# A down-projection with seven of 22 row-block pairs in Strassen's seven-product scheme, and the first norm's scale and shift during the up-projection

## The chip, the cores and the metric

One core of one Trainium2 chip runs one hybrid decoder layer for 256 tokens of 2048 channels. The metric is the time of one execution in microseconds (us) on the device. TensorE is written PE, VectorE DVE, ScalarE ACT, GpSimd POOL; SP issues most transfers.

## The reference, cut to what matters

The part of the layer that the change touches is its second half:

```python
x = layer_norm(DN_ALPHA * x + mix, ln1_g[l], ln1_b[l])
x = layer_norm(DN_ALPHA * x + conv_ffn(x, w_up[l], conv_w[l], conv_b[l], w_down[l]), ln2_g[l], ln2_b[l])
...
def layer_norm(x, g, b):
    ...
    y = (xf - mu) * lax.rsqrt(var + LN_EPS) * g + b

def conv_ffn(x, w_up, conv_w, conv_b, w_down):
    h = x @ w_up
    ...                      # acc: causal depthwise convolution of width 3 on h
    a, b = jnp.split(acc, 2, axis=-1)
    return (jax.nn.silu(a) * b) @ w_down
```

The tokens are 2 halves of 128. w_up is 2048 x 11264, w_down 5632 x 2048, all in float32.

## The kernel before, in words

Every product is made of three matmuls on parts with fewer mantissa bits: a number is split into hi and lo (`split`: ACT writes hi by a copy, DVE writes lo = value - hi), and the product is x_hi w_hi + x_hi w_lo + x_lo w_hi. Weights come from HBM in transfers of 1 MB on SP's queue into `raw` (2 buffers). `pieces` yields them in halves of 1024 columns per partition: ACT writes `whi` (line L70), DVE `wlo` (L74), 4 buffers each, and PE multiplies. The order of PE's instructions is the order of the code. Those of ACT, DVE, POOL and SP are put in order by a scheduler when the program is built, with a priority for what stands under `hp()`; at run time each engine takes its instructions strictly in that order. In the stretch around the first norm the order of ACT and DVE is the written one.

The stages at the end of the program:

- First norm and its turn (about 843 to 860 us): `ln1_turn` transposes 512 columns of the normalised x1 on PE, applies scale and shift along the partitions, and writes hi (ACT) and lo (DVE, `ln1_low`) into x1T, the operand of the up-projection. PE meanwhile does the first block of the up-projection in halves, and has to have the lo of (token half 1, part c) before it can do the matmuls of part c.
- Up-projection (to about 1340 us): 22 values of j, two products of 256 columns each (`feat_major`), then the convolution (`cv`), silu, and the split of the result into `aT`.
- Down-projection (1340 to 1580 us): four blocks of 512 columns (`tok_major`). In each, 44 row blocks of 128 are taken two to a piece; each row block takes 2 token halves x 3 matmuls of 512 columns. In the last block the last 12 row blocks are first done for token half 0, and then for token half 1 in two steps of 256 columns (`ENDS`), so that the second norm of half 0 lies beside the matmuls of half 1.
- x1 in its row form needs the first norm's scale and shift too, since it is added in the second norm. At the start of the down-projection two transfers of 1 MB on POOL's queue bring them to all partitions (`gb1`), and 8 multiplications and 8 additions of 128 x 512 on DVE apply them. Two more transfers of 1 MB bring those of the second norm (`g2`).
- `gb1` and `g2` lie in the memory of x1T (tiles x1T1 and x1T0), which is free when the last matmul of the up-projection is done.

## Time and profile before

| | |
|---|---|
| median of 3 runs | 1592.53 us (1592.27 to 1593.0) |
| the profiled execution's own time | 1593.32 us |
| its span in the trace | 1591.2 us |
| PE busy | 1576.0 us, 99% of the span |
| DVE busy | 1006.1 us, 63% |
| ACT busy | 835.9 us, 53% |
| read from HBM | 301.71 MB, 191 GB/s over the span |

The span is what the hardware profiler recorded from the first instruction to the last; the execution's own time is 2.1 us longer. Busy shares are of the span. An instruction's duration on PE and DVE overlaps that of the next a little, so the cost of one in a chain is the distance between two starts.

### The profile page before, as it was taken

The page shows a single profiled execution, that of the slowest core. Times are in us where ns is not written, and L with a number is a line of the kernel's source. Part 1 is how long each engine was busy: PE and PEld are TensorE (multiplying, and loading weights), DVE is VectorE, ACT ScalarE, POOL GpSimd, SP SyncE. Part 2 cuts the span into 40 slices and gives each one's busy share as a digit, 9 for nine tenths or more (in the row PEclk, how much of TensorE's full clock was granted, in tenths as well). Part 3 has the DMA queues.
Part 4 walks back from the last instruction along what each step waited for, and adds up shares of the span by engine and source line. Part 5 has one row for each costly group of instructions (what it writes and reads, how often), then busy time and mean ns, then how long its engine had stood idle before and what let it go on. Part 6 is the DMA issues. An engine that isn't in the chain of part 4 may idle for free.

```text
span 1591.2 us, 20296 instructions
## 1 busy us (share of the span) xinstructions
PE 1576.0 (99%) x8129; PEld 1343.7 (84%) x8129; DVE 1006.1 (63%) x1214; ACT 835.9 (53%) x986; POOL 30.2 (2%) x100
## 2 busy tenths in 40 slices
PE   9999999999999999999999999999999999999997
PEld 7888888888888888888889888888888888888886
DVE  5776547765448766447566666667666766654455
ACT  5555448546458555444447555555555555434332
POOL 1200000000000000000000000000000000000001
PEclk9999999999999999999999999999999999999999
...
GB/s 249 233 185 198 186 187 170 199 184 160 187 186 182 189 181 170 200 185 185 238 212 126 193 194 191 195 188 186 185 186 192 193 193 273 207 193 201 187 188 129
DMA packets 215645, 305.10 MB, mean 192 GB/s; under 512 B 5116, under 2 KB 133684, under 8 KB 215040
## 3 DMA queue, kind: packets, MB, share of 16 engines
...
HBM read 301.71 MB, written 2.10 MB: 191 GB/s over the span
## 4 chain that ended last, share of the span: by engine, by line
PE 97%; DMA 1%; DVE 1%; ACT 0%; SPq 0%; issue 0%
PE mm L108 30%; PE mm L150 17%; PE mm L151 16%; PE mm L149 16%; PE mm L111 15%; PE ax L554 1%; DMA raw<-in_w_out_dram 1%; PE mm L132 1%; DMA y<-in_w_in_dram 1%; DVE x L67 0%; PE mm L134 0%; PE ax L736 0%; PE ax L516 0%; DVE klo L74 0%; PE ax L425 0%; PE ax L672 0%
## 5 line engine op out<-in xcount | busy, mean ns | idle before, releaser
L74 DVE TENSOR_TENSOR wlo<-raw,whi 128x1024 fp32r<-128x1024 f32 x538 | 653.9, 1221 | 512.5 <-ACT whi L70 511.6
L70 ACT ACTIVATE whi<-raw 128x1024 fp32r<-128x1024 f32 x538 | 564.9, 1056 | 649.3 <-PE mm L151 264.3
L108 PE MATMUL mm<-x1T,whi 128*128 128x512 f32 x1376 | 432.2, 395 | 0.0
L111 PEld LDWEIGHTS mm<-x1T,wlo 128*128 128x128 f32 x1376 | 258.5, 188 | 61.1
L111 PE MATMUL mm<-x1T,wlo 128*128 128x256 f32 x1376 | 270.3, 278 | 0.0
L149 PE MATMUL mm<-whi,X 128*128 128x512 f32 x608 | 237.9, 391 | 0.0
L151 PE MATMUL mm<-whi,X 128*128 128x512 f32 x608 | 236.6, 389 | 0.0
L150 PE MATMUL mm<-wlo,X 128*128 128x512 f32 x608 | 236.6, 389 | 0.0
L108 PEld LDWEIGHTS mm<-x1T,whi 128*128 128x128 f32 x1376 | 209.4, 189 | 0.0
L108 PE MATMUL mm<-X,whi 128*128 128x512 f32 x640 | 201.9, 397 | 1.3 <-DVE X L74 1.3
L111 PEld LDWEIGHTS mm<-X,wlo 128*128 128x128 f32 x640 | 120.2, 188 | 28.4
L149 PE MATMUL mm<-whi,aT 128*128 128x512 f32 (+1 forms) x352 | 135.2, 384 | 0.0
L150 PE MATMUL mm<-wlo,aT 128*128 128x512 f32 (+1 forms) x352 | 135.2, 384 | 0.0
L151 PE MATMUL mm<-whi,aT 128*128 128x512 f32 (+1 forms) x352 | 135.2, 384 | 0.0
L151 PEld LDWEIGHTS mm<-whi,X 128*128 128x128 f32 x608 | 114.1, 188 | 23.9
L150 PEld LDWEIGHTS mm<-wlo,X 128*128 128x128 f32 x608 | 114.2, 188 | 23.1
L149 PEld LDWEIGHTS mm<-whi,X 128*128 128x128 f32 x608 | 114.2, 188 | 23.1
L111 PE MATMUL mm<-X,wlo 128*128 128x256 f32 x640 | 125.9, 278 | 0.0
L108 PEld LDWEIGHTS mm<-X,whi 128*128 128x128 f32 x640 | 97.8, 189 | 2.0 <-DVE X L74 1.7
L149 PEld LDWEIGHTS mm<-whi,aT 128*128 128x128 f32 x352 | 66.1, 188 | 13.2
L151 PEld LDWEIGHTS mm<-whi,aT 128*128 128x128 f32 x352 | 66.1, 188 | 13.2
L150 PEld LDWEIGHTS mm<-wlo,aT 128*128 128x128 f32 x352 | 66.1, 188 | 12.9
...
## 6 DMA issues: line engine op xcount, KB each, us to landing
raw<-in_w_in_dram SPq DMA_DIRECT2D x100, 1024.0 KB, 5.0
raw<-in_w_up_dram SPq DMA_DIRECT2D x88, 1024.0 KB, 5.1
raw<-in_w_down_dram SPq DMA_DIRECT2D x44, 1024.0 KB, 5.1
raw<-in_w_out_dram SPq DMA_DIRECT2D x16, 1024.0 KB, 5.1
raw<-in_w_pool_proj_dram SPq DMA_DIRECT2D x8, 1024.0 KB, 5.1
raw<-in_w_sg_proj_dram SPq DMA_DIRECT2D x8, 1024.0 KB, 5.1
raw<-in_w_hg_proj_dram SPq DMA_DIRECT2D x8, 1024.0 KB, 5.0
y<-in_w_in_dram SPq DMA_DIRECT2D x3, 1024.0 KB, 13.0
```

The source lines that it names most:

```text
L70: nc.scalar.activation(out=o, in_=a, func=f, **kw)
L74: low.tensor_tensor(out=lo, in0=src, in1=hi.bitcast(F32), op=ALU.subtract)
L108: nc.tensor.matmul(ps[:, c, :], lhsT=hi[:, k, c * P:(c + 1) * P], rhs=xT(kt)[:, 0:512], start=kt == 0, stop=False)
L111: nc.tensor.matmul(ps[:, c, 0:256], lhsT=lo[:, k, c * P:(c + 1) * P], rhs=xT(kt)[:, 0:256], start=False, stop=kt == kt_n - 1)
L132: nc.tensor.matmul(pv[:, :, ts], lhsT=hi[:, k, cs], rhs=xv[:, :, ts], start=kt == 0, stop=False)
L149: nc.tensor.matmul(o[:, w], lhsT=xT(kt)[:, xs], rhs=hi[:, k, w], start=kt == first, stop=False)
L150: nc.tensor.matmul(o[:, w], lhsT=xT(kt)[:, xs], rhs=lo[:, k, w], start=False, stop=False)
L151: nc.tensor.matmul(o[:, w], lhsT=xT(kt)[:, xl], rhs=hi[:, k, w], start=False, stop=kt == kt_n - 1)
L554: nc.tensor.matmul(tp[:, hc], lhsT=ke[:, hc], rhs=qe[:, hc], start=True, stop=True)
```

## The change: what it does

The down-projection is done in two quads of 1024 columns. Two row blocks of weights (k = 0, 1) by two halves of columns (h = 0, 1) are a pair: a 2 x 2 block matrix, multiplied by the 2 x 2 block matrix of activations (2 token halves by 2 row blocks). A plain pair takes 8 block products of 3 matmuls, 24 in all. The 7 pairs in `FAST` take 7 products, 21 matmuls, in each quad, with sums of activations (`mix_tokens`, made once, in the first quad) and sums of weights (`tt`, in each quad). Three of the seven products and one more are gathered in accumulators of their own (`e`) and added to x1 by `drain`; the rest go straight into the accumulators of the result (`c`), which `settle` adds to x1. `ORDER0` and `ORDER1` say in which order PE takes the pairs. The first quad has all 22 pairs; the second has 16 by this scheme and the last 12 row blocks as before, with the same ending by `ENDS`. A pair's weights are 1 MB; a third place for them, `wide[:, 1]`, and the place of the weights' sums, `wide[:, 0]`, lie in x1T1. The activations' sums lie in x1T0 for four pairs and in a new pool for three, so `g2` can be loaded into x1T0 only when PE is done with the fourth fast pair (pair 6) in the second quad.

The scale and shift of x1 are now written in the up-projection, for j = 4 to 11, in 8 slices of 256 columns with two transfers of 128 KB on POOL's queue and four DVE operations each, in one buffer `gb`.

```diff
+TAIL = 16
+FAST = (0, 2, 4, 6, 8, 10, 12)
+ORDER0 = (1, 3, 0, 5, 7, 2, 9, 11, 4, 13, 14, 6, 15, 16, 8, 17, 18, 10, 19, 12, 20, 21)
+ORDER1 = (1, 0, 3, 2, 5, 4, 7, 6, 9, 8, 11, 10, 13, 12, 14, 15)
...
+    def ln1_affine(i):
+        cs = slice(256 * i, 256 * (i + 1))
+        gb = pas.tile([P, 2, 256], F32, name="gb", bufs=1)
+        nc.gpsimd.dma_start(out=gb[:, 0, :], in_=ln1_g[0, cs].partition_broadcast(P))
+        nc.gpsimd.dma_start(out=gb[:, 1, :], in_=ln1_b[0, cs].partition_broadcast(P))
+        for t in range(NT):
+            mul(x1[:, t, cs], x1[:, t, cs], gb[:, 0, :])
+            add(x1[:, t, cs], x1[:, t, cs], gb[:, 1, :])
...
     for j in range(KF // 2):
+        if 4 <= j < 12:
+            ln1_affine(j - 4)
...
-    g2 = ff.tile([P, 2, D], F32, name="x1T0")
-    gb1 = ff.tile([P, 2, D], F32, name="x1T1")
-    nc.gpsimd.dma_start(out=gb1[:, 0, :], in_=ln1_g[0].partition_broadcast(P))
-    nc.gpsimd.dma_start(out=gb1[:, 1, :], in_=ln1_b[0].partition_broadcast(P))
-    for c in range(4):
-        cs = slice(512 * c, 512 * (c + 1))
-        for t in range(NT):
-            mul(x1[:, t, cs], x1[:, t, cs], gb1[:, 0, cs])
-            add(x1[:, t, cs], x1[:, t, cs], gb1[:, 1, cs])
...
-    for j in range(3):
-        cs = slice(512 * j, 512 * (j + 1))
-        ps = tok_major(wdown, 512 * j, aT, KF)
...
+    def mix_tokens(p):
+        with hp():
...
+            add(work[:, 0:512].rearrange("p (j c) -> p j c", j=2), av[:, :, 0:S], av[:, :, S:2 * S])
+            sub(sm[:, 1, :], full[:, 0, 0, :], full[:, 0, 1, :])
+            sub(sm[:, 0, :], full[:, 1, 1, :], full[:, 0, 1, :])
+            add(sm[:, 2, :], full[:, 0, 0, :], sm[:, 0, :])
+            sub(sm[:, 3, :], full[:, 1, 0, :], sm[:, 2, :])
+            to = S_of(p)
+            split(to[:, 0], to[:, 1], sm)
...
+    def quarters(p, cb):
...
+            if i % 3 == 2:
+                raw = wide[:, 1].rearrange("p (k h) c -> p k (h c)", k=2)
+            else:
+                raw = wst.tile([P, 2, 1024], F32, name="raw", bufs=RAW_BUFS)
+            nc.sync.dma_start(out=raw, in_=wdv[:, 2 * p:2 * p + 2, cb:cb + 1024])
...
+    def plain_pair(p, cb, c):
+        q = quarters(p, cb)
+        for j in range(2):
+            w2, w1 = both(q[:, 2 * j:2 * j + 2, :])
+            for i in range(NT):
+                x = act_of(p, j, i)
+                c[i, 2].go(x, w2)
+                c[i, 1].go(x, w1)
+
+    def fast_pair(p, cb, c, e):
...
+        b11, b22 = both(q[:, 1:3, :])
+        with hp():
+            tt = wide[:, 0]
+            add(tt[:, 0:2, :], q[:, 1:3, :], q[:, 0:1, :].broadcast_to([P, 2, 512]))
+            add(tt[:, 2, :], tt[:, 0, :], q[:, 2, :])
+            add(tt[:, 3, :], tt[:, 2, :], q[:, 3, :])
+        e[1].go(act_of(p, 0, 0), b11)
+        c[0, 2].go(s4, b22)
+        b21, = both(q[:, 3:4, :], 1)
+        c[0, 1].go(act_of(p, 1, 0), b21)
+        t1, t3 = both(tt[:, 0:2, :])
+        e[5].go(s5, t1)
+        e[7].go(s7, t3)
+        t2, t4 = both(tt[:, 2:4, :])
+        e[6].go(s6, t2)
+        c[1, 1].go(act_of(p, 1, 1), t4)
...
+    def settle(cb, t, n, ps):
+        with hp():
+            v = at(cb, t, n)
+            add(v, v, ps)
+            nc.vector.bn_stats(out=st2[:, t, cb // 512 + 2 - n, :], in_=v)
...
+            if p in FAST:
+                fast_pair(p, cb, c, e)
+                todo -= 1
+                if not quad and todo:
+                    mix_tokens(FAST[NF - todo])
+                if not todo:
+                    drain(cb, e)
+            else:
+                plain_pair(p, cb, c)
+        if not quad:
+            for t in range(NT):
+                for n in (2, 1):
+                    settle(cb, t, n, c[t, n].ap)
+    g2 = ff.tile([P, 2, D], F32, name="x1T0")
```

Where the scheduler put the instructions is seen in the built programs. Names carry buffer numbers; line numbers differ between the two programs (lo was L74 and is L78, subtraction L58 and L62, addition L61 and L65, multiplication L64 and L68).

**The first norm's turn, on DVE.** Before, in the stretch where DVE makes the lo parts of token half 1 for x1T (parts 0, 1, 2 and 3; `full` is a transposed part) and goes on to the lo of the weights:

```order
L58 TENSOR_TENSOR x1T0_5969<-full_6534,x1T0_5969 128x4x128
L58 TENSOR_TENSOR x1T0_5969<-full_6560,x1T0_5969 128x4x128
L64 TENSOR_TENSOR full_6588<-ax_6583,vcol_386 128x512
L61 TENSOR_TENSOR full_6588<-full_6588,vcol_386 128x512
L58 TENSOR_TENSOR x1T1_5970<-full_6588,x1T1_5970 128x4x128
L58 TENSOR_TENSOR x1T1_5970<-full_6614,x1T1_5970 128x4x128
L74 TENSOR_TENSOR wlo_6640<-raw_6637,whi_6639 128x1024
L74 TENSOR_TENSOR wlo_6660<-raw_6637,whi_6659 128x1024
```

Now, from the same lo of part 0 to that of part 2 (gb_7613 and gb_7818 are the second and third slice of scale and shift; DMASW is a transfer of POOL's queue):

```order
L62 TENSOR_TENSOR x1T0_5969<-full_6534,x1T0_5969 128x4x128 [waits Activation_49]
L68 TENSOR_TENSOR x1_5971<-x1_5971,gb_7613 128x256 [waits DMASW2_49]
L68 TENSOR_TENSOR x1_5971<-x1_5971,gb_7613 128x256
L65 TENSOR_TENSOR x1_5971<-x1_5971,gb_7613 128x256 [waits DMASW3_49,DVE_49]
L65 TENSOR_TENSOR x1_5971<-x1_5971,gb_7613 128x256 [waits DVE_49]
L62 TENSOR_TENSOR x1T0_5969<-full_6560,x1T0_5969 128x4x128 [waits Activation_49]
L68 TENSOR_TENSOR full_6588<-ax_6583,vcol_386 128x512 [waits PE_49]
L65 TENSOR_TENSOR full_6588<-full_6588,vcol_386 128x512 [waits DVE_49]
L68 TENSOR_TENSOR x1_5971<-x1_5971,gb_7818 128x256 [waits DMASW4_49]
L68 TENSOR_TENSOR x1_5971<-x1_5971,gb_7818 128x256
L65 TENSOR_TENSOR x1_5971<-x1_5971,gb_7818 128x256 [waits DMASW5_49,DVE_49]
L62 TENSOR_TENSOR x1T1_5970<-full_6588,x1T1_5970 128x4x128 [waits Activation_49]
```

The multiplications and additions of x1 stand between the lo parts, each group behind a wait for its transfers. The remaining lo of part 3 has the last addition of gb_7818 ahead of it, and the two wlo have the multiplications of the fourth slice (gb_8023) ahead of them; the fifth slice's stand two wlo further on.

On POOL, the transfers of the second, third and fourth slice:

```order
L838 DMA gb_7613<-in_ln1_g_dram 128x256 [waits DMASW1_49,DMASW0_49,DVE_49]
L839 DMA gb_7613<-in_ln1_b_dram 128x256 [waits DMASW3_49]
L838 DMA gb_7818<-in_ln1_g_dram 128x256 [waits DMASW3_49,DMASW4_49,DMASW2_49,DVE_49]
L839 DMA gb_7818<-in_ln1_b_dram 128x256 [waits DMASW5_49]
L838 DMA gb_8023<-in_ln1_g_dram 128x256 [waits DMASW5_49,DMASW6_49,DMASW4_49,DVE_49]
```

The first transfer of each slice waits for DVE: for the last addition of the slice before it, since there is one buffer.

**The start of the down-projection, on DVE.** Before, from the last convolution of the up-projection on (x1T1 is here scale and shift):

```order
L67 SCALAR_TENSOR_TENSOR cv_10957<-h_10952,ccol_929,cv_10957 128x256 x4
L74 TENSOR_TENSOR wlo_11061<-raw_11058,whi_11060 128x1024
L64 TENSOR_TENSOR cv_10860<-cv_10860,cv_10957 128x512
L74 TENSOR_TENSOR wlo_11077<-raw_11058,whi_11076 128x1024
L74 TENSOR_TENSOR aT21_6706<-cv_10860,aT21_6706 128x2x256
L64 TENSOR_TENSOR x1_5971<-x1_5971,x1T1_10970 128x512 x2
L74 TENSOR_TENSOR wlo_11095<-raw_11092,whi_11094 128x1024
L61 TENSOR_TENSOR x1_5971<-x1_5971,x1T1_10970 128x512 x2
```

Now, behind the last convolution there stand the first addition of `tt` (1024 columns, which waits for a transfer), the multiplication of cv and the wlo of pair 0's first two weights, and then the following (x1T1 is here `wide`, `work` the sums of activations, and the last row is the lo of the first activations' sums, for pair 0):

```order
L78 TENSOR_TENSOR aT21_6706<-cv_10920,aT21_6706 128x2x256 [waits Activation_49]
L65 TENSOR_TENSOR x1T1_11035<-x1T1_11035 128x512
L65 TENSOR_TENSOR work_11034<-aT0_6685 128x512 [waits DVE_49]
L65 TENSOR_TENSOR x1T1_11035<-x1T1_11035 128x512 [waits DVE_49]
L62 TENSOR_TENSOR work_11034<-work_11034 128x128 [waits DVE_49]
L62 TENSOR_TENSOR work_11034<-work_11034 128x128
L78 TENSOR_TENSOR wlo_11131<-x1T1_11035,whi_11130 128x512 [waits PE_49]
L65 TENSOR_TENSOR work_11034<-work_11034 128x128 [waits DVE_49]
L78 TENSOR_TENSOR wlo_11138<-x1T1_11035,whi_11137 128x1024 [waits Activation_49]
L62 TENSOR_TENSOR work_11034<-work_11034 128x128 [waits DVE_49]
L78 TENSOR_TENSOR wlo_11148<-x1T1_11035,whi_11147 128x1024 [waits Activation_49]
L78 TENSOR_TENSOR x1T0_11032<-work_11034,x1T0_11032 128x512 [waits Activation_49]
```

The lo of pair 0's activation sums stands behind four wlo and all sums of pair 0's weights. On SP the transfer of pair 0's weights into x1T1 waits for PE, for the last matmul of the up-projection.

**Between the two quads, on DVE.** Here mm_11037 holds the sums of token half 0 and mm_11038 those of half 1, mm_11036 is one of the accumulators `e`; the first two additions belong to `settle`:

```order
L78 TENSOR_TENSOR wlo_11945<-x1T1_11035,whi_11944 128x1024 [waits DMAHW5_49,Activation_49]
L65 TENSOR_TENSOR x1_5971<-x1_5971,mm_11037 128x512 [waits DVE_49,PE_49]
L65 TENSOR_TENSOR x1_5971<-x1_5971,mm_11037 128x512
L1041 BN_STATS st2_6707<-x1_5971 128x6 [waits DVE_49] x2
L78 TENSOR_TENSOR wlo_11958<-x1T1_11035,whi_11957 128x512 [waits Activation_49]
L71 SCALAR_TENSOR_TENSOR x1_5971<-x1_5971,x1T1_11035 128x512
L65 TENSOR_TENSOR x1T1_11035<-x1T1_11035 128x1024 [waits DVE_49]
L62 TENSOR_TENSOR x1_5971<-x1_5971,mm_11036 128x512
L65 TENSOR_TENSOR x1T1_11035<-x1T1_11035 128x512 [waits DVE_49]
L65 TENSOR_TENSOR x1_5971<-x1_5971,mm_11038 128x512 [waits DVE_49,PE_49]
L65 TENSOR_TENSOR x1_5971<-x1_5971,mm_11038 128x512
L1041 BN_STATS st2_6707<-x1_5971 128x6 [waits DVE_49] x2
```

Behind these rows stand one more addition of `tt` and then wlo_11965, the lo of the second quad's first `tt`. The first matmul of the second quad writes into the buffer of mm_11037, so it waits for the first two additions. Before, four blocks of 512 columns followed each other with other buffers ready.

## Rows read from the trace of the kernel before

**Rows 1.** The page: busy time by engine, and the chain that ended last, by engine.

```profile
PE 1576.0 (99%) x8129; PEld 1343.7 (84%) x8129; DVE 1006.1 (63%) x1214; ACT 835.9 (53%) x986; POOL 30.2 (2%) x100
...
PE 97%; DMA 1%; DVE 1%; ACT 0%; SPq 0%; issue 0%
```

**Rows 2.** Windows: stretch, length, busy us (instructions) of PE, PEld, DVE, ACT, POOL; clock, DMA share, GB/s.

```profile
16.00:18.00 2.00, 1.36 (x7) 1.18 (x8) 2.00 (x3) 0.66 (x3) 0.00 (x0) 1.00 1.06 388
840.00:860.00 20.00, 20.00 (x165) 19.25 (x163) 12.59 (x22) 16.14 (x34) 0.64 (x3) 1.00 0.31 103
1340.00:1360.00 20.00, 20.00 (x91) 16.56 (x90) 14.25 (x20) 9.30 (x11) 1.07 (x2) 1.00 0.81 303
1400.00:1450.00 50.00, 50.00 (x223) 41.38 (x222) 24.45 (x22) 20.07 (x19) 0.00 (x0) 1.00 0.57 198
1580.00:1583.00 3.00, 0.03 (x1) 0.00 (x0) 2.83 (x7) 0.12 (x1) 0.99 (x1) 1.00 0.27 93
1583.00:1585.00 2.00, 0.00 (x0) 0.00 (x0) 1.97 (x3) 0.60 (x1) 1.32 (x1) 0.87 0.34 128
```

**Rows 3.** Timeline of PE in the down-projection: start, duration, operation; and its last matmul.

```profile
1340.02 0.40 PE L149 MATMUL mm<-whi,aT 128*128 128x512 f32 x1
...
1349.78 0.39 PE L150 MATMUL mm<-wlo,aT 128*128 128x512 f32 x1
...
1579.75 0.28 PE L151 MATMUL mm<-whi,aT 128*128 128x256 f32 x1
```

**Rows 4.** Timeline of DVE in the first norm's turn; in brackets idle time before, and releaser.

```profile
848.17 0.69 DVE L58 TENSOR_TENSOR x1T<-full,x1T 128x512 fp32r<-128x512 f32 x1
848.77 0.69 DVE L64 TENSOR_TENSOR full<-ax,vcol 128x512 f32<-128x512 f32 x1
...
850.88 0.69 DVE L58 TENSOR_TENSOR x1T<-full,x1T 128x512 fp32r<-128x512 f32 x1 [0.70 <-ACT x1T L70]
853.13 0.69 DVE L58 TENSOR_TENSOR x1T<-full,x1T 128x512 fp32r<-128x512 f32 x1 [1.56 <-ACT x1T L70]
...
858.86 4.63 DVE L74 TENSOR_TENSOR wlo<-raw,whi 128x1024 fp32r<-128x1024 f32 x4 [0.26 <-ACT whi L70]
```

**Rows 5.** Timeline of PE there: the starts of parts 0 and 1, and the first L111.

```profile
852.83 0.36 PE L132 MATMUL mm<-x1T,whi 128*128 128x256 f32 x1
...
855.08 0.36 PE L132 MATMUL mm<-x1T,whi 128*128 128x256 f32 x1
...
861.18 0.40 PE L111 MATMUL mm<-x1T,wlo 128*128 128x256 f32 x2
```

**Rows 6.** DMA issues: queue, count, KB each, median us from issue to landing.

```profile
raw<-in_w_down_dram SPq DMA_DIRECT2D x44, 1024.0 KB, 5.1
...
x1T<-in_ln_g_dram POOLq DMA_DIRECT2D x2, 1024.0 KB, 6.3
...
t<-in_sg_b_dram POOLq DMA_DIRECT2D x1, 512.0 KB, 4.2
...
lv<-in_lv_mask_dram POOLq DMA_DIRECT2D x2, 256.0 KB, 3.1
...
rampt<-in_ramp_dram POOLq DMA_DIRECT2D x1, 32.0 KB, 4.4
```

**Rows 7.** Groups of DVE by form: 128 x 256 of two tensors; busy, mean ns.

```profile
L58 DVE TENSOR_TENSOR lv<-t,t 128x256 f32<-128x256 f32 x28 | 10.6, 421 | 0.0
```

**Rows 8.** Timeline of DVE at the start of the down-projection.

```profile
1343.71 1.93 DVE L67 SCALAR_TENSOR_TENSOR cv<-h,ccol,cv 128x256 f32<-128x256 f32 x4 [0.74 <-ACT cv L70]
...
1348.24 0.68 DVE L64 TENSOR_TENSOR cv<-cv 128x512 f32<-128x512 f32 x1
```

**Rows 9.** Timeline of ACT there, with the waits for weights.

```profile
1346.00 2.01 ACT L70 ACTIVATE whi<-raw 128x1024 fp32r<-128x1024 f32 x2 [1.90 <-DMA raw<-in_w_down_dram]
...
1363.00 2.01 ACT L70 ACTIVATE whi<-raw 128x1024 fp32r<-128x1024 f32 x2 [5.25 <-DMA raw<-in_w_down_dram]
```

More of the change, by code (lines that the diff above doesn't have):

```diff
@@ L909, in ln2_last @@
             else:
[L910 removed]
+                add(x1[:, t, 1536:2048], x1[:, t, 1536:2048], ps)
             i = 3 + (c0 > 0)
@@ new lines, in hybrid_layer, with tail_act @@
+    nc.gpsimd.dma_start(out=g2[:, 1, :], in_=ln2_b[0].partition_broadcast(P))
+    rest = wdown[2 * TAIL * P:, :]
+    kt_n = KF - 2 * TAIL
+    def tail_act(k, i):
+        return act_of(TAIL + k // 2, k % 2, i)
+    for k0, n, hi, lo in pieces(rest, 1024, 512, kt_n, 4, 2):
+        for k in range(n):
+            for t in range(NT):
+                c[t, 2].go(tail_act(k0 + k, t), (hi[:, k, :], lo[:, k, :]))
+    for t in range(NT):
+        settle(1024, t, 2, c[t, 2].ap)
+    kept = []
+    for k0, n, hi, lo in pieces(rest, 1536, 512, kt_n, 4, 2, home=tail_home):
+        kept.append((k0, n, hi, lo))
+        for k in range(n):
+            c[0, 1].go(tail_act(k0 + k, 0), (hi[:, k, :], lo[:, k, :]))
@@ L928, in hybrid_layer @@
+    ln2_last(0, c[0, 1].ap, 0, 512)
+    c0 = 0
+    for c1 in ENDS:
+        o = Sum(extra[0], kt_n) if c0 else c[1, 1]
+        for k0, n, hi, lo in kept:
+            for k in range(n):
+                w = slice(c0, c1)
+                o.go(tail_act(k0 + k, 1), (hi[:, k, w], lo[:, k, w]), w)
+        ln2_last(1, o.ap, c0, c1)
+        c0 = c1
+    dn_cm.__exit__(None, None, None)
     up_cm.__exit__(None, None, None)
```

99 lines of the change are left out of this document (86 added, 13 removed).

## The prediction, as recorded before the changed kernel ran

> **What bounds the kernel now.** I read the page first: PE is busy for 99% of the span, and the chain of work that ended last lies on PE for 97% [rows 1]. So the end moves by what PE is spared and by what PE is made to wait, and by nothing else. The windows then say whether one stage differs: in the down-projection PE fills every stretch at a granted clock of 1.00, while DVE is busy for 24.45 of 50 us and the DMA engines for 0.57; in the first 20 us of that stage, with four transfers of 1 MB on POOL's queue, DVE has 14.25 of 20 and the DMA share is 0.81 [rows 2]. Even there PE does not wait, though ACT waited 5.25 us for weights [rows 9]. The last matmul starts at 1579.75 [rows 3]; the 11.2 us behind it are the second norm's end, and the change keeps that.
>
> **What is removed from PE.** The stage's matmuls of 512 columns start 0.2267 us apart: 1340.02 to 1349.78 is 43 steps [rows 3]. Seven fast pairs save 3 matmuls in each of two quads, 7 x 3 x 2 = 42, so PE is spared 42 x 0.2267 = 9.5 us. Nothing else in PE's count changes. The 16 affine operations of 512 columns taken out of the down-projection lie on DVE beside busy PE, and the four transfers likewise, so I give their removal nothing.
>
> **What is added, place by place.** DVE's prices are distances of starts: 512 columns 0.60 (848.17 to 848.77), 1024 columns 1.13 (four in 4.63) [rows 4], 256 columns about 0.33 (0.42 less the same overlap) [rows 7], and about 0.2 for 128 columns, an estimate by the same line.
>
> *The first norm's turn.* The scheduler took the first affine slices out of the middle of the up-projection and put them between the lo parts that PE waits for. There is one buffer, so slice n+1 is fetched only after DVE's last addition of slice n, and DVE, in order, stands waiting meanwhile. POOL's transfers took 3.1 us for 256 KB and 4.2 for 512 KB [rows 6]; by that line 128 KB take 2.6, an estimate. The second transfer is issued about 0.55 behind the first. Now the walk. Behind the lo at 848.17 stand three small operations, one of 512 and one small: slice 1's last use ends at 850.85. The lo of part 0 then comes 1.2 later than its 850.88, which ends as PE wants it, at 852.83 [rows 4, 5]. A round costs 0.1 + 2.6 + 0.55 + 0.05 and two additions, 0.66: slice 2's last use 854.8, the lo of part 1 ends at 855.5 where PE wants it at 855.08 [rows 5]. In the next round a lo stands between the additions: 859.4. Then the fourth slice's multiplications, which stand ahead of the first wlo: 859.4 + 2.75 + 0.66 = 862.8, and the wlo is there at 864.0 where its L111 stood at 861.18 [rows 5]. The stall is 2.9 us. From then on DVE has four wlo ready-made work ahead of PE and the remaining slices fit, with about 1 us to spare. The term is three times the landing time, nearly: 2.2 us a transfer would give 1.7, and 4.4, as the 32 KB transfer took [rows 6], 8.3. I take 2.9, since the 256 KB row is of the same kind and nearest.
>
> The Trainium skill ("DMA: Bandwidth & Descriptors", section "Anatomy of one DMA — SWDGE (gpsimd) path") gives about 2.0 us fixed plus the bytes over 436 GB/s for a transfer from this queue. By it 128 KB take 2.3 us and the term would be 2.0, an estimate; for 256 KB it says 2.6 where this trace shows 3.1, so I stay with the row.
>
> *The start of the first quad.* Pair 0's weights go into x1T1, free when the last matmul of the up-projection is done, at about 1340.2, just behind the first one of the down-projection [rows 3]. With 5.1 us [rows 6] they land at 1345.3. DVE's last convolutions end at 1345.6 [rows 8]. Then, in the order shown: addition of 1024 (1.13), cv (0.60), wlo (1.13), lo of aT21, addition, work, addition (4 x 0.60), two small (0.4), wlo of 512 (0.60), small, wlo of 1024, small (1.5), wlo of 1024 (1.13), and the lo of the activation sums, 0.7: it is there at 1355.2. PE reaches it 53 matmuls into the stage, at 1340.2 + 53 x 0.2267 = 1352.2. The hi, two matmuls earlier, is bound by the same chain. So PE waits 3.1 us. The bounds are 2.0 (the small ones cost nothing, the 1024s overlap) and 5.0 (weights landing 9 us after their issue, as a transfer beside 1 MB loads did when ACT waited 1.90 and 5.25 [rows 9], while DVE's earlier work is done).
>
> *Inside the first quad.* Two plain pairs and a fast one keep PE for 69 x 0.2267 = 15.6 us; DVE needs about 13.2 (8 wlo of 1024 and one of 512, additions of weights 2.3, activation sums 2.0). That fits, but wlo for the seventh product, the next pair's addition and the next plain wlo stand close: slack is about 0.1 us, four times. Between 0 and 2; I take 0.5, nearer to nothing since PE waits nowhere while DVE has a fifth of its time free [rows 2].
>
> *Between the quads.* The first matmul of the second quad waits for two additions of `settle`, which can start only 6 matmuls (1.4 us) before the quad's end and stand behind a wlo of 1024: 1.1 us late. Behind them DVE has nine operations, about 9.0 us, ahead of wlo_11965, which PE wants 34 matmuls (7.7 us) into the quad: 1.3 more. Together 2.4; 1.1 to 3.4 by whether that wlo has started in time.
>
> *Inside the second quad.* One plain and one fast pair: PE 45 x 0.2267 = 10.2 us, DVE about 8.6. But the third weights place is a loop: wlo of the pair there, transfer 5.1 [rows 6], addition, wlo of 1024, wlo of 512, the next pair's wlo, about 10.3. I take 0.4 for the quad, 0 to 2.
>
> *g2.* Two transfers of 1 MB now start after pair 6 of the second quad, beside this loop. A 1 MB transfer on POOL's queue took 6.3 us [rows 6], and weights beside four of them came late by up to 5.25 us [rows 9]. Two of them make pair 10's weights late by about half of that; against the buffers 1.8 us reach PE, 0 to 3.4.
>
> *The last blocks.* A matmul waits for one `settle` addition: 0.3.
>
> **Sum.** Stalls 2.9 + 3.1 + 0.5 + 2.4 + 0.4 + 1.8 + 0.3 = 11.4, less 9.5: +1.9 us. The profiled execution took 1593.3, 0.8 over the median, and would take 1595.2; on the median's footing 1592.5 + 1.9 = **1594.4 us**. All terms low give 5.1 and 1588.1; all high give 24 and 1607, and neither is likely together. 0.2%, 3.2 us, is about what can be told from no change.
>
> **Rivals.** *(A) PE is covered, 1583 to 1589.* If the transfers land in about 2.2 us and the start and the change of quads cost 1 us each, because DVE's small operations overlap better than by their distances, stalls are about 5 and the time 1588; with none it is 1583. For it: PE waits nowhere in the stage before, behind wlo buffers four deep. Against it: the three places wait on an event (a landing, a last matmul), where more buffers of weights don't help.
>
> *(B) The POOL round trips are long, 1600.* At 4.4 us a landing the first norm's term is 8.3 and the time 1599.8. It is the mechanism that puts the result on the slower side by itself; it decides from a landing of about 3.1 us on. For it: the 32 KB transfer, far smaller, took 4.4 [rows 6]. Against: that was near the start, where the DMA share is about 1 (1.06 at 16 to 18 us); from 840 to 860 us it is 0.31 [rows 2].
>
> *(C) The second quad is bound by its loop, 1600.* If the loop is 0.6 us longer than PE's 10.2 for seven fast pairs, it costs 4.2 instead of 0.4, and g2 its 3.4. For it: the loop and PE differ by less than the reading of one transfer. Against: the two other weights places keep a pair ahead.
>
> *(D) The clock falls, 1598.* At the end of the trace the granted clock is 1.00 (2.4 GHz) for 3 us behind the last matmul and 0.87 in the next two; with PE idle for 0.64 of 2 us, at 16 to 18 us, it kept 1.00 [rows 2]. Stalls of 3 us lie between these. If it fell at both long stalls and came back after 4 us of work at 1.2 GHz, that adds 2 us each. The Trainium skill ("TensorE: Matmul & The Clock Gate", section "Part 1: The HAM clock gate (the "warmup" mystery)") says that an idle TensorE drops to half clock and needs sustained work to regain it; the end of the trace agrees, and no row shows it with work waiting.
>
> **How the numbers follow.** The forecast, 1590.5 to 1598, has 0.52; A 0.17; B 0.11; C 0.13; D 0.07. The range 1588.5 to 1600 leaves out most of A, and what of B and C goes beyond. Faster than 1589.3: A, 0.17 with a little of the forecast's edge. Slower than 1595.7: B, C, D (0.31) and the forecast's upper part. The rest is within 0.2%.
>
> **What the profile would show.** PE's count lower by 42 matmuls of 512; idle PE of about 3 us near 861 with DVE's rows before it waiting on POOL's transfers gb, one landing apart; idle of about 3 us near 1352 released by ACT's and DVE's parts of x1T0; two gaps at the quads' border, 1.1 and 1.3; DVE's idle rising around them. I am wrong if the affine rows near 855 show no wait, if the landing of 128 KB is far from 2.6, or if PE has many small gaps in the second quad in place of these few.

## The result, and the profile after

The changed kernel takes 1618.33 us (median of 4 runs, 1617.35 to 1621.6), the kernel before 1592.76 beside it: a ratio of 1.0164, 95% interval 1.0147 to 1.0182. It is slower by 25.6 us; 1594.4 was forecast, at most 1600. The profiled span grew by 25.8, from 1591.2 to 1617.0.

The page of the changed kernel: busy time, the granted clock in 40 slices, and the chain by engine.

```profile
PE 1578.6 (98%) x8087; PEld 1342.4 (83%) x8087; DVE 1084.8 (67%) x1358; ACT 859.9 (53%) x1023; POOL 38.8 (2%) x114
...
PEclk9999999999999999999998999999999999999999
...
PE 88%; DMA 6%; DVE 4%; issue 1%; ACT 1%; SPq 0%; POOL 0%; DVEq 0%; ACTq 0%; POOLq 0%
```

PE's work is smaller by the 42 matmuls, 8087 for 8129 in [rows 1], yet its chain fell from 97% to 88%: DMA has 6% and DVE 4% of it. PE's busy time grew though its work shrank, and one slice of the clock row is an 8. So time went in two ways, by waiting and by work at a lower clock.

The timeline of PE: every wait of 0.3 us and more from the first norm to the end, with its releaser in brackets.

```profile
858.08 0.38 PE L136 MATMUL mm<-x1T,whi 128*128 128x256 f32 x1 [1.94 <-DVE x1T L62]
...
863.80 0.58 PE L136 MATMUL mm<-x1T,whi 128*128 128x256 f32 x1 [3.02 <-DVE x1T L62]
...
886.68 0.50 PE L115 MATMUL mm<-x1T,wlo 128*128 128x256 f32 x2 [1.78 <-DVE wlo L78]
...
894.84 0.51 PE L115 MATMUL mm<-x1T,wlo 128*128 128x256 f32 x2 [2.30 <-DVE wlo L78]
...
903.66 0.80 PE L115 MATMUL mm<-x1T,wlo 128*128 128x256 f32 x2 [2.97 <-DVE wlo L78]
...
1373.51 0.50 PE L959 MATMUL mm<-whi,x1T 128*128 128x512 f32 x1 [2.69 <-ACT x1T L74]
...
1374.58 0.75 PE L961 MATMUL mm<-whi,x1T 128*128 128x512 f32 x1 [0.34 <-DVE x1T L78]
...
1480.92 0.47 PE L959 MATMUL mm<-whi,aT 128*128 128x512 f32 x1 [1.03 <-DVE x L65]
...
1489.80 0.51 PE L960 MATMUL mm<-wlo,x1T 128*128 128x512 f32 x1 [0.89 <-DVE wlo L78]
...
1537.14 0.51 PE L960 MATMUL mm<-wlo,mixed 128*128 128x512 f32 x1 [3.88 <-DVE wlo L78]
...
1588.85 0.47 PE L959 MATMUL mm<-x1T,aT 128*128 128x512 f32 x1 [1.03 <-DVE x L65]
```

The first five rows are in the first norm's turn and the beginning of the up-projection, 12.0 us in all; [rows 5] had none there. The first two wait for the lo of parts 1 and 2 of x1T, the next three for the lo of weights (`wlo`). The next two are the start of the first quad, then the quads' border (1.03 and 0.89), g2 (3.88) and the last block (1.03).

Windows of the changed kernel (columns as in [rows 2]): a wait, the stretch behind the next wait, one a little later, and two behind the wait at 1373.51.

```profile
856.00:858.00 2.00, 0.13 (x2) 0.00 (x0) 1.74 (x6) 0.00 (x0) 0.29 (x1) 1.00 0.01 2
864.00:866.00 2.00, 2.00 (x11) 2.00 (x11) 0.68 (x2) 0.00 (x0) 1.06 (x2) 0.50 0.13 27
870.00:872.00 2.00, 2.00 (x14) 1.78 (x13) 2.00 (x4) 1.55 (x2) 0.00 (x0) 1.00 0.03 8
1376.00:1377.00 1.00, 1.00 (x4) 0.82 (x3) 0.50 (x1) 0.77 (x2) 0.00 (x0) 0.50 0.07 29
1380.00:1381.00 1.00, 1.00 (x6) 0.85 (x5) 1.00 (x1) 1.00 (x2) 0.00 (x0) 1.00 0.67 135
```

At 864 to 866 us PE is busy for the whole stretch, at a granted clock of 0.50 (1.2 GHz): 11 matmul records, where 14 stand at 1.00. The same at 1376. The rows of PE there show what it costs: two matmuls of 512 columns 0.43 us apart, for 0.2267 in [rows 3].

```profile
1375.55 0.63 PE L960 MATMUL mm<-wlo,aT 128*128 128x512 f32 x1
...
1375.98 0.63 PE L961 MATMUL mm<-whi,aT 128*128 128x512 f32 x1
```

One form of matmul shows when the clock fell the first time: it takes 0.34 us at 859.05 and 0.52 at 859.30. That is 1.2 us after the wait of 1.94 us had ended, and before the wait of 3.02 began.

```profile
859.05 0.34 PE L136 MATMUL mm<-x1T,whi 128*128 128x256 f32 x1
...
859.30 0.52 PE L136 MATMUL mm<-x1T,whi 128*128 128x256 f32 x1
```

Timeline of DVE where it stands behind the slices' transfers; then POOL's issues of the transfers of scale for the second, third and fifth slice.

```profile
855.64 0.76 DVE L68 TENSOR_TENSOR x<-x,gb 128x256 f32<-128x256 f32 x2 [2.07 <-DMA gb<-in_ln_g_dram]
...
861.45 0.76 DVE L68 TENSOR_TENSOR x<-x,gb 128x256 f32<-128x256 f32 x2 [2.10 <-DMA gb<-in_ln_g_dram]
...
877.10 0.76 DVE L68 TENSOR_TENSOR x<-x,gb 128x256 f32<-128x256 f32 x2 [4.16 <-DMA gb<-in_ln_g_dram]
...
892.89 0.76 DVE L68 TENSOR_TENSOR x<-x,gb 128x256 f32<-128x256 f32 x2 [4.00 <-DMA gb<-in_ln_g_dram]
```

```profile
851.87 0.58 POOL L838 DMA_DIRECT2D gb<-in_ln_g_dram  x1 [4.80 <-DVE x L65]
...
857.71 0.54 POOL L838 DMA_DIRECT2D gb<-in_ln_g_dram  x1 [4.72 <-DVE x L65]
...
872.10 0.54 POOL L838 DMA_DIRECT2D gb<-in_ln_g_dram  x1 [6.66 <-DVE x L65]
```

The walk of the forecast is there, step by step: issue, landing, two multiplications, an addition, the next issue. But a slice's transfer of scale takes about 3.7 us from issue to landing when nothing else is fetched (851.87 to 855.64) and 5.0 beside weights (872.10 to 877.10). The issues by kind (count, KB, median us to landing; the medians are over all eight slices):

```profile
gb<-in_ln_g_dram POOLq DMA_DIRECT2D x8, 128.0 KB, 4.1
...
gb<-in_ln_b_dram POOLq DMA_DIRECT2D x8, 128.0 KB, 4.4
...
x1T<-in_ln_b_dram POOLq DMA_DIRECT2D x1, 1024.0 KB, 8.9
```

The share of each stage follows from the first and the last matmul of the down-projection. They start at 1340.02 and 1579.75 before [rows 3], at 1359.07 and 1605.61 after. So 19.1 us are lost ahead of the down-projection, and 6.8 in it, where 9.5 were to be spared.

### The profile page after: what moved, and what is told of

Read it like the earlier page. It is cut to its first block, busy times and chain, and to the rows that moved or that the text cites. A ratio compares the mean times of both kernels' runs of the same rounds, so it can differ in the third digit from the quotient of the medians.

```text
span 1617.0 us, 20447 instructions
## 1 busy us (share of the span) xinstructions
PE 1578.6 (98%) x8087; PEld 1342.4 (83%) x8087; DVE 1084.8 (67%) x1358; ACT 859.9 (53%) x1023; POOL 38.8 (2%) x114
## 3 DMA queue, kind: packets, MB, share of 16 engines
q8 instruction: 63, 1.03, 0.3%
## 4 chain that ended last, share of the span: by engine, by line
PE 88%; DMA 6%; DVE 4%; issue 1%; ACT 1%; SPq 0%; POOL 0%; DVEq 0%; ACTq 0%; POOLq 0%
PE mm L112 29%; PE mm L115 14%; PE mm L155 11%; PE mm L154 11%; PE mm L153 11%; PE mm L961 2%; PE mm L960 2%; PE mm L959 2%; DMA raw<-in_w_down_dram 2%; DVE wlo L78 2%; PE ax L558 1%; DMA gb<-in_ln_b_dram 1%; DMA raw<-in_w_out_dram 1%; DMA x1T<-in_w_down_dram 1%; DMA y<-in_w_in_dram 1%
## 5 line engine op out<-in xcount | busy, mean ns | idle before, releaser
L78 DVE TENSOR_TENSOR wlo<-raw,whi 128x1024 fp32r<-128x1024 f32 (+1 forms) x514 | 619.4, 1214 | 413.4 <-ACT whi L74 412.4
L74 ACT ACTIVATE whi<-raw 128x1024 fp32r<-128x1024 f32 (+1 forms) x514 | 535.4, 1050 | 537.5 <-PE mm L112 191.2
L74 ACT ACTIVATE whi<-x1T 128x1024 fp32r<-128x1024 f32 (+1 forms) x52 | 50.9, 986 | 77.9 <-PE mm L961 42.6
L959 PE MATMUL mm<-whi,aT 128*128 128x512 f32 (+1 forms) x219 | 85.3, 389 | 1.0 <-DVE x L65 1.0
L960 PE MATMUL mm<-wlo,aT 128*128 128x512 f32 (+1 forms) x219 | 85.7, 391 | 0.2 <-DVE wlo L78 0.2
L961 PE MATMUL mm<-whi,aT 128*128 128x512 f32 (+1 forms) x219 | 85.2, 389 | 0.0
L153 PE MATMUL mm<-whi,y 128*128 128x512 f32 x192 | 75.5, 393 | 0.0
L155 PE MATMUL mm<-whi,y 128*128 128x512 f32 x192 | 74.9, 390 | 0.0
```

The costliest lines, as they stand in the source:

```text
L74: nc.scalar.activation(out=o, in_=a, func=f, **kw)
L78: low.tensor_tensor(out=lo, in0=src, in1=hi.bitcast(F32), op=ALU.subtract)
L153: nc.tensor.matmul(o[:, w], lhsT=xT(kt)[:, xs], rhs=hi[:, k, w], start=kt == first, stop=False)
L155: nc.tensor.matmul(o[:, w], lhsT=xT(kt)[:, xl], rhs=hi[:, k, w], start=False, stop=kt == kt_n - 1)
L959: nc.tensor.matmul(o, lhsT=xh, rhs=wh, start=self.fresh, stop=False)
L960: nc.tensor.matmul(o, lhsT=xh, rhs=wl, start=False, stop=False)
```

## The experiments

Ratios are to the kernel before, measured beside each run (1592.3 us, within 0.2). Where a run is said to start or end its down-projection at a time, that is the first or last matmul row of its own trace.

**1. The slices in the middle of the up-projection.**

```diff
-        gb = pas.tile([P, 2, 256], F32, name="gb", bufs=1)
+        gb = pas.tile([P, 2, 256], F32, name="cv", bufs=4)
...
-            cv = pas.tile([P, 2, S], F32, name="cv", bufs=3)
+            cv = pas.tile([P, 2, S], F32, name="cv", bufs=4)
```

> The changed kernel, but gb takes its place among the cv buffers (four instead of three, and no buffer of its own), so that a slice can be fetched only when the convolution four tiles before is done and its operations stand in the middle of the up-projection. Theory 1 (the scale and shift cost 18.5 us, because DVE stands behind one landing for each slice, and PE's clock falls in the longest waits): no idle PE between 850 and 910 us, granted clock 1.00 there, time about 1600 us, 18 less than the changed kernel. Rival (the 32 operations and their transfers cost DVE and DMA time wherever they stand): the waits move to where the slices now stand, and the time stays within 5 us of 1618.

1613.58 us, ratio 1.0132 (1.0115 to 1.0148). PE waits nowhere between 840 and 950 us, and the clock is 1.00. But the down-projection starts at 1354.07: 14 of the 19 us are lost in another place. Theory 1 was right on the stretch from 840 to 950 us and wrong on the time; the rival's time held, 4.8 us under 1618.3, and its waits did move to where the slices stand. PE waits at the last six of the eight slices; at the first two it doesn't. PE's rows at one slice, ACT's row ahead of them, and windows (2 us in which the slice's transfers run, and the stretch with the second to the eighth slice):

```profile
1019.26 0.73 PE L112 MATMUL mm<-x1T,whi 128*128 128x512 f32 x2 [0.61 <-ACT whi L74]
...
1020.53 0.50 PE L115 MATMUL mm<-x1T,wlo 128*128 128x256 f32 x2 [0.53 <-DVE wlo L78]
...
1024.18 0.50 PE L115 MATMUL mm<-x1T,wlo 128*128 128x256 f32 x2 [0.59 <-DVE wlo L78]
```

```profile
1018.15 1.06 ACT L74 ACTIVATE whi<-raw 128x1024 fp32r<-128x1024 f32 x1 [6.65 <-DMA raw<-in_w_up_dram]
```

```profile
1010.00:1012.00 2.00, 2.00 (x14) 1.73 (x13) 1.89 (x2) 1.50 (x3) 0.24 (x1) 1.00 0.69 52
950.00:1150.00 200.00, 190.62 (x1069) 161.63 (x1068) 134.34 (x196) 99.55 (x134) 9.22 (x30) 1.00 0.62 186
```

ACT stood 6.65 us for weights issued at 1009.62. They landed 8.4 us later; 5.1 is usual. At 1010 to 1012 us, where hardly any of their data moves yet, the DMA engines are busy at a share of 0.69 and move 52 GB/s. PE is idle for 9.4 of 200 us. The 14.2 us lost are more, since the matmuls around a wait start further apart by more than its idle time: the wait of 0.61 at 1019.26 delays its matmul by 0.78 us and the next by another 0.10, against the same instructions in run 10, where PE has no wait there.

**2. That part alone, in the kernel before.**

```diff
+    def ln1_affine(i):
+        ...
+        gb = up.tile([P, 2, 256], F32, name="gb", bufs=1)
...
+        if 4 <= j < 12:
+            ln1_affine(j - 4)
...
-    gb1 = ff.tile([P, 2, D], F32, name="x1T1")
...
```

> The kernel before, with one part of the change alone: scale and shift of x1 in eight slices of 256 columns for j = 4 to 11 with one buffer gb, and without the two 1 MB transfers and 16 operations at the start of the down-projection. Theory 1: the scheduler takes the slices to the first norm's turn here too, and the time rises by about 18 us, to 1611, with PE idle 12 to 13 us between 850 and 910 us and some 10 us at half clock. Rival (the stalls come with the new pools and the rest of the change): less than 8 us.

1608.8 us, ratio 1.0104 (1.0089 to 1.0119), 16.4 us slower. Its down-projection takes as long as before (239.72 us for 239.73); the loss is all ahead of it, in five waits between 877 and 923 us, 11.1 us in all, and two stretches at half clock. Theory 1 has the time (1611 expected), but not the place: the turn itself is undisturbed here. Three of the waits, and two windows:

```profile
879.14 0.50 PE L111 MATMUL mm<-x1T,wlo 128*128 128x256 f32 x2 [1.84 <-DVE wlo L74]
...
897.91 0.51 PE L111 MATMUL mm<-x1T,wlo 128*128 128x256 f32 x2 [1.95 <-DVE wlo L74]
...
914.04 0.51 PE L111 MATMUL mm<-x1T,wlo 128*128 128x256 f32 x2 [2.71 <-DVE wlo L74]
```

```profile
899.50:901.50 2.00, 2.00 (x8) 1.71 (x8) 2.00 (x5) 1.03 (x2) 1.00 (x2) 0.50 1.05 372
914.50:916.50 2.00, 2.00 (x14) 1.73 (x13) 2.00 (x5) 1.87 (x3) 0.95 (x2) 1.00 0.56 190
```

The wait of 1.95 us was followed by half clock, the longer one of 2.71 was not.

So this part alone costs 16.4 us, about two thirds of the result, without any of Strassen's scheme.

**3. g2 later.**

```diff
-        return mixed[i // 4][:, i % 4]
+        return mixed[0][:, i - 3] if i > 2 else mixed[1][:, i]
```

> The changed kernel with the first three fast pairs' activation sums in the new pool and the last four in x1T0, so that g2 can be loaded only after the last fast pair (pair 12) of the second quad. Theory 1 (g2's two transfers delay the weights of pair 10): the wait of 3.9 us near 1533 us and the low clock behind it go, and nothing comes in their place in the tail, where weights are two transfers ahead: 5 to 6 us less, about 1612. Rival (the second quad's loop over the third weights place waits anyway): a wait of 1 us or more at each fast pair stays, and the time within 2 us of 1618.

1616.35 us (one run). The wait of 3.88 us is gone, and 2.0 us of waiting with low clock behind it came in the tail:

```profile
1565.80 0.50 PE L959 MATMUL mm<-whi,aT 128*128 128x512 f32 x1 [1.25 <-ACT whi L74]
...
1567.06 0.80 PE L960 MATMUL mm<-wlo,aT 128*128 128x512 f32 x1 [0.76 <-DVE wlo L78]
```

The down-projection lasts 245.55 us, 1.0 less. Neither expectation held whole: theory 1 is right that the wait goes, wrong that nothing comes in its place; the rival has the time, but no wait at each fast pair. So at this second place the two transfers cost nearly as much as at the first.

**4. The first activation sums ahead.**

```diff
-    def mix_tokens(p):
-        with hp():
+    def mix_tokens(p, work):
+        with hp(1 + (p == FAST[0])):
...
-            mix_tokens(FAST[0])
+            mix_tokens(FAST[0], wide[:, 0].rearrange("p a c -> p (a c)")[:, 1024:2048])
```

> The changed kernel with the first pair's activation sums made in wide instead of work and at a higher priority, so that they stand ahead of the last convolution and of the sums of weights on DVE. Theory 1 (PE waits at the start of the first quad for these sums, since they stand behind four wlo): the waits of 2.7 and 0.3 us near 1371 us and the low clock behind them go, 5.3 us less, about 1613. Rival (the weights in wide, which land 5 us after the up-projection's end, are what is late): a wait of 2 to 3 us stays there, now released by wlo of pair 0.

1614.68 us (one run). There is no wait of PE between 910 and 1475 us in its timeline, and the down-projection lasts 243.01 us, 3.5 less. The time is 3.7 us lower for the 5.3 expected. The theory holds for the waits: they go, and no wait for wlo of pair 0 comes in their place.

**5. Half the transfers, rows of 2 KB.**

```diff
-        gb = pas.tile([P, 2, 256], F32, name="gb", bufs=1)
-        nc.gpsimd.dma_start(out=gb[:, 0, :], in_=ln1_g[0, cs].partition_broadcast(P))
-        nc.gpsimd.dma_start(out=gb[:, 1, :], in_=ln1_b[0, cs].partition_broadcast(P))
+        src, op = ((ln1_g, mul), (ln1_b, add))[i % 2]
+        nc.gpsimd.dma_start(out=gb, in_=src[0, cs].partition_broadcast(P))
...
```

> As the first run of this study (slices placed by the cv buffers), but eight transfers of 256 KB with rows of 2 KB (for each 512 columns first the scale, then the shift) instead of sixteen of 128 KB with rows of 1 KB: the same bytes, half the packets, one transfer per step. Theory 3, formed from the first run (a broadcast in rows of 1 KB keeps the DMA engines busy while it moves little, so the next weights land 3 us late and PE waits about 2 us at each slice): PE's waits between 990 and 1130 us fall to less than half, time about 1604 to 1607. Rival (it is the bytes, or DVE's operations between the wlo): the same 11 to 13 us are lost, 1613.

1614.14 us, ratio 1.0134 (1.0119 to 1.0149), as in the first run, so theory 3 fell in this form. One transfer takes longer to land in return, 5.6 us for 256 KB. The expected "half the packets" did not come about, as the pages show. Here are the transfers, and the DMA queues (packets, MB, share of 16 engines' span) of runs 1, 5 and 10; q0 is POOL's queue, q1 SP's, and run 10 (below) has no slices to fetch:

```profile
cv<-in_ln_g_dram POOLq DMA_DIRECT2D x4, 256.0 KB, 5.6
```

```profile
q1 hardware_dynamic: 204192, 296.77, 54.6%
q0 software_dynamic: 2112, 7.06, 2.1%
...
q0 software_dynamic: 1984, 7.06, 1.8%
...
q0 software_dynamic: 1344, 4.96, 0.9%
```

The slices are 768 packets in run 1 and 640 in run 5, so the run halves the number of transfers and doubles the rows in the program, but takes only a sixth of the packets away. From the same rows: the 2.10 MB of the slices hold 1.2% of run 1's span on 16 engines and 0.9% of run 5's, an estimate of 149 and 112 us of one engine's time for each MB, where SP's weights need 47. The engines are held about three times as long for a byte of these slices as for one of the weights, and longer rows cut that by a quarter without giving any time back.

**6. Scale and shift back in the down-projection.**

```diff
-        if 4 <= j < 12:
-            ln1_affine(j - 4)
...
+    gb1 = ff.tile([P, 2, D], F32, name="x1T1")
+    nc.gpsimd.dma_start(out=gb1[:, 0, :], in_=ln1_g[0].partition_broadcast(P))
...
-            if i % 3 == 2:
+            if i > 6 and i % 3 == 2:
...
+ORDER0 = (1, 3, 5, 7, 9, 0, 11, 2, 13, 14, 4, 15, 6, 16, 17, 8, 18, 10, 19, 12, 20, 21)
```

> The changed kernel with scale and shift of x1 again at the start of the down-projection, by two transfers of 1 MB into x1T1 and 16 operations of 512 columns; the first five pairs are plain, and the third place for weights is used from the ninth pair on. Strassen's part stays whole. If the move of the scale and shift is what costs (16 to 18 us), and the late activation sums at the start 5 us, the time is before (1592.4) less 9.5, plus what is left in the down-projection: the quads' border 2.4, small waits 1, g2 5.9, the last block 1.2: about 1593, within 3. Rival (the seven-product scheme itself costs more than it spares, by DVE's and DMA's load): 1600 or more.

1609.0 us, ratio 1.0104 (1.0089 to 1.0119). The 19 us ahead of the down-projection are gone (it starts at 1338.57), but a new wait of this version's own came in. PE's row, and DVE's last operation of scale and shift with the next addition of weights:

```profile
1377.17 0.79 PE L955 MATMUL mm<-whi,x1T 128*128 128x512 f32 x1 [9.19 <-ACT whi L74]
```

```profile
1373.54 0.67 DVE L65 TENSOR_TENSOR x<-x,x1T 128x512 f32<-128x512 f32 x1
...
1374.74 1.20 DVE L65 TENSOR_TENSOR x1T<-raw 128x1024 f32<-128x1024 f32 x1
```

The weights' sums lie in x1T1 too, and could not be written before scale and shift had been read for the last time. The time is the rival's (1600 or more), but the cause is this wait and not the load that the rival named. So this run says that the move is what costs the 19 us ahead of the down-projection, and leaves open what Strassen's part gives.

**7. No fast pairs.** This one leaves out the scaling of x1 by alpha, which stands in `drain` for all 2048 columns.

```diff
-FAST = (0, 2, 4, 6, 8, 10, 12)
+FAST = ()
```

> The changed kernel with FAST empty: all 22 pairs plain, no sums, no drain; the eight slices of scale and shift stay in the up-projection, the quads and their end as changed. Theory 1: affine part 16 to 18 us, border and last block 1 to 2, no saving: 1610 to 1613, so the seven-product scheme as it stands costs 5 to 8 us net although it spares PE 9.5. Rival (the fast pairs bring their 9.5 us): 1625 or more.

1612.01 us, ratio 1.0123 (1.0108 to 1.0138). The down-projection takes 241.13 us with no fast pair and 246.54 with seven in each quad, though these have 9.5 us less work for PE: 14.9 us are lost again with them, most of it in waits (10.1 us idle) and at low clock. The time is as theory 1 had it.

**8. Run 6 with two repairs.**

```diff
-            places = [pa[:, 0, :], pa[:, 1, :], pb, pc]
+            places = [pb, pc, pa[:, 0, :], pa[:, 1, :]]
...
+        if k0 == 4:
+            for a, v in enumerate((ln2_g, ln2_b)):
+                nc.gpsimd.tensor_copy(out=g2[:, a, 0:1], in_=hi.bitcast(F32)[:, 0, 0:1])
+                nc.gpsimd.dma_start(out=g2[:, a, :], in_=v[0].partition_broadcast(P))
```

> As the sixth run, and also: g2 loaded only when the second half of the tail's first four row blocks is split (a small copy on POOL into g2 waits for it), and in the second quad the sums of token half 0 in the two small PSUM tiles, those of half 1 in the big one, so that its first matmul does not wait for settle. If the waits named are what is lost: 1592.4 - 9.5 + 1.2 (border, second gap) + 1 (small) = about 1585, with g2's wait gone and no clock fall; 1583 to 1588. Rival (g2's wait only moves to the tail, as in the third run): 1589 to 1592 with a wait of 2 to 3 us near the end.

1604.06 us, ratio 1.0076 (1.0059 to 1.0093), 4.9 under run 6. The waits at g2 and at the border's first matmul are gone; the border's second grew from 0.89 to 2.11 us, and that of 9.9 us at the first fast pair stands. The expected 1585 overlooked it.

**9 and 10. Only the transfers, only the operations.** Both start from run 1.

```diff
-        for t in range(NT):
-            mul(x1[:, t, cs], x1[:, t, cs], gb[:, 0, :])
-            add(x1[:, t, cs], x1[:, t, cs], gb[:, 1, :])
```

```diff
-        nc.gpsimd.dma_start(out=gb[:, 0, :], in_=ln1_g[0, cs].partition_broadcast(P))
-        nc.gpsimd.dma_start(out=gb[:, 1, :], in_=ln1_b[0, cs].partition_broadcast(P))
+        nc.gpsimd.memset(gb, 1.0)
```

> As the first run of this study (slices placed by the cv buffers), without the 32 multiplications and additions that read them: the sixteen transfers are still made. It leaves out the first norm's scale and shift of the rows of x1. Theory 3 in its second form (a slice's 256 KB hold up the weights that are fetched at the same time by about 3 us, whatever the rows' length, and PE has buffers for about one of these): the waits of about 2 us at each slice stay, and the time within 3 us of 1613.6. Rival (DVE's operations between the wlo are what is late): the waits go, about 1600.

> As the first run of this study, with the sixteen transfers replaced by a memset of each slice on POOL: the 32 operations stay in place. It puts 1 for scale and shift. Theory 3 in its second form: no waits between 950 and 1150 us, about 1600. Rival (DVE's operations): 1610 or more.

1606.77 us, ratio 1.0086 (1.0071 to 1.0102), and 1598.97, ratio 1.0041 (1.0027 to 1.0055). The window of run 1 over the second to the eighth slice, for run 9 and for run 10:

```profile
950.00:1150.00 200.00, 195.30 (x1106) 167.80 (x1106) 128.79 (x172) 103.36 (x138) 9.36 (x31) 1.00 0.63 192
```

```profile
950.00:1150.00 200.00, 200.00 (x1151) 174.51 (x1150) 146.59 (x208) 113.32 (x144) 5.04 (x25) 1.00 0.57 190
```

With the operations alone PE is never idle there; with the transfers alone it is for 4.7 us, with both for 9.4. From the first matmul of the up-projection to that of the down-projection the loss against the kernel before is 0.0, 7.6 and 14.2 us. So the transfers hold up the weights, and the operations cost nothing alone but nearly double the loss when they come with the transfers. That they do so by standing between the wlo that have to catch up is in line with the rows (the third wait of a slice, at 1024.18 in run 1, is missing in run 9), and was not tested by itself. The expectation for run 9, waits of 2 us and 1613.6, was too high; that for run 10 came true. Its 6.6 us over the kernel before are in its down-projection, which takes 246.50 us like that of the changed kernel.

**11. Scale and shift of the first norm in x1T0.**

```diff
-    gb1 = ff.tile([P, 2, D], F32, name="x1T1")
+    gb1 = ff.tile([P, 2, D], F32, name="x1T0")
...
-            if i > 6 and i % 3 == 2:
+            if i % 3 == 2:
...
+ORDER1 = (1, 3, 0, 5, 2, 7, 4, 9, 6, 11, 8, 13, 10, 14, 12, 15)
```

> As the eighth run, but with the scale and shift of the first norm loaded into x1T0 instead of x1T1, so that the sums of weights (in x1T1) need not wait for their last use; the last four pairs' activation sums take x1T0 later; the third place for weights is free from the start; and the second quad begins with two plain pairs. If the wait of 9.9 us at the first fast pair, with the low clock behind it, came from x1T1 alone: it goes, as does most of the 2.1 us at the border; 1604.1 less 12 to 16: 1586 to 1591, faster than before. Rival (the transfers of 2 MB at that place hold up the weights of the first pairs): a wait of 3 us or more near 1365 us, 1593 or more.

1593.03 us, ratio 1.0002 (0.9993 to 1.0011): 11 us under run 8, and level with the kernel before. The 9.9 us are gone, so x1T1 was their cause, and the rival's wait of 3 us near 1365 did not come; but the time is the rival's, and 1586 to 1591 was missed. The down-projection lasts 239.90 us: the waits that are left (1.25 and 0.82 at the first fast pair, 0.64 at 1515, 1.43 and 0.76 where g2 is loaded, and six under 0.3) are 5.6 us of idle PE, and with the late starts of the matmuls around them they still eat the 9.5.

**12. The first fast pair and g2 a little later.**

```diff
+ORDER0 = (1, 3, 5, 7, 9, 11, 0, 13, 2, 14, 15, 4, 16, 6, 17, 8, 18, 10, 19, 12, 20, 21)
...
     for k0, n, hi, lo in pieces(rest, 1536, 512, kt_n, 4, 2, home=tail_home):
         kept.append((k0, n, hi, lo))
+        if k0 == 4:
+            ...
```

> As the eleventh run, with the first fast pair one place later in the first quad (six plain pairs ahead of it, then fast pairs at every second or third place), and g2 loaded only when the second four row blocks of the last 512 columns are split, with one transfer of weights still to come. If the eleventh run's waits came from where these two stand (2.6 us at the first fast pair, beside the 16 operations of scale and shift on DVE, and 2.8 at g2 in the tail), 4 to 5 us go: 1593.0 less 4 to 5, 1588 to 1589, faster than before by 0.2 to 0.3%. Rival (DVE is too full in the first quad and g2 now holds up the last weights or is late for the second norm): 1592 or more.

1590.7 us (1589.33 to 1593.55), ratio 0.9989 (0.998 to 0.9998): 1.7 us under the kernel before, the only version here that beats it, by less than the 0.2% named ahead and between the two expectations (1588 to 1589, 1592 or more). g2's waits are gone; those at the first fast pair stayed, though the pair is later:

```profile
1375.19 0.49 PE L955 MATMUL mm<-whi,mixed 128*128 128x512 f32 x1 [0.56 <-ACT whi L74]
...
1376.52 0.50 PE L956 MATMUL mm<-wlo,mixed 128*128 128x512 f32 x1 [0.83 <-DVE wlo L78]
...
1378.99 0.50 PE L956 MATMUL ax<-wlo,mixed 128*128 128x512 f32 x1 [0.81 <-DVE wlo L78]
```

## Why the prediction was wrong, step by step

**Where the 24 us beyond the forecast lie.** Ahead of the down-projection 2.9 us were forecast and 19.1 lost: against run 10, start to start, the two waits in the turn cost 5.5, the three later ones 7.6, and slow matmuls behind the waits, most at half clock, 5.5; half a us lies before the up-projection's first matmul. In the down-projection 1.0 was to be won (8.5 of stalls less 9.5) and 6.8 were lost.

**The mechanism at the first norm was right, its size was not.** The first step that failed is "by that line 128 KB take 2.6, an estimate", and with it the "2.9 us" of the first norm's term. In the turn the scale landed in 3.3 to 3.8 us and the shift in 3.9 to 4.4; over all slices the medians are 4.1 and 4.4. The place was a little off as well: the walk had the stall at the first wlo, the profile has it at the lo of parts 1 and 2, and none at the first wlo. Rival B had the mechanism and priced it at 8.3 for 4.4 us a landing; the two waits came to 5.0, and B's time, 1599.8, lacks the later slices and the clock as the forecast does. The line through 256 and 512 KB was no good guide: the 32 KB row in [rows 6], set aside as near the start of the program, was nearer, and the page before has more of its kind, smaller transfers that take longer than 256 KB:

```profile
lv<-in_conv_w_dram POOLq DMA_DIRECT2D x3, 44.0 KB, 6.0
```

The fit from the Trainium skill ("DMA: Bandwidth & Descriptors", section "Anatomy of one DMA — SWDGE (gpsimd) path"), 2.3 us for this size, is further off still.

**"The remaining slices fit, with about 1 us to spare" failed too, and cost more.** This is the term that was put at nothing. The waits at 886.68, 894.84 and 903.66, 7.05 us, belong to the later slices, where each transfer runs beside weights: that of scale lands in 4.5 to 5.1 us instead of 3.7, and DVE, in order, stands before it with the wlo behind: for 4.00 us ahead of the row at 892.89, with PE's wait at 894.84 for the wlo that follows, and for 2.08 and 2.66 us ahead of the other two. The weights issued there landed in 5.0 to 5.6 us, so here it is DVE that was late, not the weights. That the reverse can hold as well, that weights land later for the slices, is shown by runs 1, 9 and 10, and no term of the sum had it. I had priced transfers by how long they take, never by what they do to the transfers beside them.

**The clock.** The sum had nothing for it. Rival D had a fall at two long waits and 4 us for both; how long the clock would stay low it took from no row. The clock fell behind the wait that ended at 858.08 and stayed at 0.50 through the next one, to 869.5 us; it fell again behind the waits at 903.66, 1373.51 and 1537.14, each time while PE had work. The sum of waits ahead of the down-projection is 12.0 us, the loss 19.1; of the rest most has its place in the rows at 0.50, but no run takes the clock alone away. From 1374.6 to 1378 us eight matmuls cost 0.2 us more each. Waits of 1.03 (1480.92) and of 1.78 and 2.30 us (886.68, 894.84) left it at 1.00. No length of a wait divides the two kinds in these runs: half clock followed waits of 1.95 (run 2), 2.11 (run 8, 1477.95) and 1.25 with 0.76 (run 3), and did not follow 2.71 (run 2) nor 1.43 with 0.76 (run 11). The Trainium skill ("TensorE: Matmul & The Clock Gate", section "Part 1: The HAM clock gate (the "warmup" mystery)") says that idle time halves the clock; at the four falls named the trace agrees, with work waiting.

**The start of the first quad** was right in place, releaser and size: 3.1 forecast, 2.69 and 0.34 waited, plus the low clock behind it; run 4 removed it by the cause named.

**Between the quads** was right in size (2.4; 1.19 and 1.05 from start to start over the usual distance) and place. That settle's buffer makes the first wait is in line with run 8, where other PSUM places leave no such row.

**Inside the quads** the small waits came to about 0.3 and 0.9 for 0.5 and 0.4, start to start; the loop of rival C did not bind.

**g2** was mis-sized: 1.8 forecast, 3.88 waited and a low clock behind, near 6 together. The weights issued beside its two transfers, at 1525.23 and 1527.58, landed after 9.4 and 9.6 us, and the wait moved with the transfers in run 3.

**The last block** cost 1.03 for 0.3.

**That 42 matmuls are worth 9.5 us** holds for PE's work, and rival A, that it comes through, failed: run 7 against the changed kernel gives 14.9 us of new losses in the down-projection. In run 12, with all repairs, 237.75 us for 239.73 before is a gain of 2.0 in this stage.

What stays open: why a byte of such a broadcast holds the DMA engines about three times as long as one of the weights. Rows of 2 KB for 1 KB did not help (run 5). Transfers that aren't broadcasts, from POOL's queue, were not tried, nor the same broadcast from SP's.
